# Four held-back weight tiles placed earlier in the load order of a hybrid attention block, a longer warm-up and a second cut tile

## The chip, the cores and the metric

The kernel runs on one core of one Trainium2 chip. The metric is the device time of one execution in microseconds; a median over several executions is given. One further execution was taken with the hardware profiler, and all rows shown here come from that one. TensorE (PE in the rows, with PEld for its weight loads) does the products, ScalarE (ACT) and VectorE (DVE) prepare operands and empty PSUM, and SyncE (SP) issues most DMAs.

## What is computed

One layer on an input `x` of 256 tokens by 2048 features, all in float32:

```python
proj = x @ w_in                                   # 2048 -> 5440 columns
ret_out = silu(rg) * groupnorm(retention(rope(rq), rope(rk), rv))
mla_out = mla(cq, ckv, kr)                        # latent attention with a block-causal mask
x = layer_norm(alpha * x + concat(ret_out, mla_out) @ w_out, ln1_g, ln1_b)
h = square(relu(x @ w_up)) @ w_down               # 2048 -> 8192 -> 2048
x = layer_norm(alpha * x + h, ln2_g, ln2_b)
```

## The kernel before

**Products.** Every product is made from operands split in two: a high part, rounded to the reduced float32 that TensorE takes in one pass, and a low part that holds the rest. Three products replace one: high by high, high by low, low by high. A weight tile comes from memory as a raw tile of 128 partitions by up to 2048 columns (1 MB); for each piece of 1024 columns ACT copies the high part (`L175`) and DVE subtracts it from the raw piece to get the low part (`L176`). These two instructions are "the split" of a piece, and a tile of 2048 columns has two pieces.

**Jobs.** `weights()` makes one job for each tile and appends it to the list `jobs`; the order of that list is the order of loads and of splits. `load_ahead()` issues loads, three raw buffers ahead (`NRAW`). `unit()` is called after each group of products and lets up to two pieces be split. Split pieces of most jobs go into five rotating slots (`NSLOT`), and such a piece is not emitted until the slot's former piece has been used. A job with `into=` puts its pieces into memory of its own and needs no slot. All of SP's loads stand in one queue in list order, and each waits until the raw buffer that it overwrites has been split.

**Start.** Five products on a zeroed tile `warm` run first (`L365`). The first stage takes 16 tiles `w_mla` of 1344 columns, numbered kt = 0 to 15, each in two pieces of 896 and 448 columns. Tile 0 alone is cut into three loads of 448 columns, the first of them issued by ACT, and its products stand in an order of their own (`L384`): all 12 with the high weights, column block by column block, then 6 with the low weights. All others go through `xstat` (`L286`), where the low weights are wanted after the first three products. Each tile takes 18 products of 448 columns. Between the weights, tiles of `x_t` are loaded and split too (`x_job`).

**Down projection.** 64 tiles `w_down`, kt = 0 to 63, against the squared activations `rhl`, which ACT and DVE split four tiles at a time in `r_split(b)` (`L876`, `L877`); batch b serves kt = 4b to 4b+3, and there are two buffers for batches. Tiles 0 to 57 (`NDOWN = 58`) run in order of kt, each with 24 products of 512 columns into all eight PSUM banks. The last six tiles, 58 to 63, are held back and run bank by bank (`down_bank`), 18 products for each bank, so that the final layer norm of one bank can overlap the products of the next. Tiles 58 to 61 have memory of their own (`staged_down`), 62 and 63 use the slots. In the list of jobs all stand in order of kt. `r_split(15)`, for tiles 60 to 63, is issued behind tile 57:

```python
        if kt % 4 == 1 and kt // 4 < 15:
            r_split(kt // 4 + 1)
```

After tile 63 two tiles with the rows of the last layer norm are loaded (`row_job(2)`, `row_job(3)`). Two such tiles for the first layer norm stand behind `w_down` tiles 8 and 16 in the list, and are used by DVE in four pieces each.

Of the kernel before, what the change touches and what calls it, by code (L numbers as in the profile page):

```python
# [14 lines left out]
P = 128  # L15
# [9 lines left out]
NMLA = 1344  # L25
# [9 lines left out]
NDOWN = 58  # L35
# [32 lines left out]
def kernel(  # L68
# [19 lines left out]
    nc = tc.nc  # L88
# [12 lines left out]
    def acc(name):  # L101
        return psum.tile([P, 512], F32, tag="acc", name=name)

    def bank(name):
        return psum.tile([P, 512], F32, tag="wk", name=name)
# [16 lines left out]
    def next_piece(force):  # L122
        while state["job"] < len(jobs) and jobs[state["job"]].emitted == len(jobs[state["job"]].pieces):
            state["job"] += 1
        if state["job"] == len(jobs):
            return False
        job = jobs[state["job"]]
        if job.slotted:
            if len(holders) >= NSLOT and not force and not holders[-NSLOT][0]:
                return False  # L130
            holders.append(job.free[job.emitted])
        load_ahead(state["job"])
        job.pieces[job.emitted]()
        job.emitted += 1
        return True

    def use(job, n=None):
        while job.emitted < (len(job.pieces) if n is None else n):
            next_piece(True)
        return Cols(job.hi, job.width), Cols(job.lo, job.width)  # L140

    def free(job, pieces=None):
        for i, f in enumerate(job.free):
            if pieces is None or i in pieces:
                f[0] = True

    def raw_tile(job, name):
        job.raw = wraw.tile([P, 2048], F32, tag="raw", name=name)
        return job.raw

    def weights(src, n, name, into=None, width=1024, cuts=None):

        job = Job(None, [], into is None)
        job.width = width
        spans = list(zip(cuts, cuts[1:])) if cuts else [(0, n)]

        def load():
            raw = raw_tile(job, f"raw_{name}")
            for i, (a, b) in enumerate(spans):
                (nc.scalar if cuts and i == 0 else nc.sync).dma_start(raw[:, a:b], src[:, a:b])  # L160

        def piece(i):
            a, m = i * width, min(width, n - i * width)
            if into is None:
                hi = wsp.tile([P, 1024], F32R, tag="hi", name=f"hi_{name}_{i}")
                lo = wsp.tile([P, 1024], F32R, tag="lo", name=f"lo_{name}_{i}")
            else:
                hi, lo = into(i)
            job.hi.append(hi)
            job.lo.append(lo)  # L170
            for o, e in spans if cuts else ((a, a + m),):
                o, e = max(o, a) - a, min(e, a + m) - a
                if o < e:
                    r = job.raw[:, a + o:a + e]
                    nc.scalar.copy(hi[:, o:e], r)  # L175
                    nc.vector.tensor_sub(lo[:, o:e], r, hi[:, o:e].bitcast(F32))  # L176

        job.load = load
        job.pieces = [lambda i=i: piece(i) for i in range((n + width - 1) // width)]
        job.free = [[False] for _ in job.pieces]  # L180
        jobs.append(job)
        return job

    def other(load, pieces):
        job = Job(None, pieces, False)
        job.load = lambda: load(job)
        job.free = []
        jobs.append(job)
        return job
# [14 lines left out]
    xhl = slab.tile([P, KT, 512], F32R, tag="slab", name="xhl")  # L204
# [4 lines left out]
    def x_job(k0, n):  # L209
        def load(job):  # L210
            nc.sync.dma_start(xraw[:, k0 * S:(k0 + n) * S], x_t[:, k0 * S:(k0 + n) * S])

        def piece():
            v = xraw[:, k0 * S:(k0 + n) * S].rearrange("p (k t) -> p k t", k=n)
            nc.vector.tensor_copy(xhl[:, k0:k0 + n, 0:S], v)
            nc.vector.tensor_sub(xhl[:, k0:k0 + n, S:], v, xhl[:, k0:k0 + n, 0:S].bitcast(F32))

        other(load, [piece]).raw_user = False
# [73 lines left out]
    x_job(0, 1)  # L292
    j_mla, j_ret, j_out = [], [], []
    for k in range(KT):
        j_mla.append(weights(w_mla[k], NMLA, f"mla{k}", width=896, cuts=(0, 448, 896, NMLA) if k == 0 else None))
        if k in X_AFTER:
            x_job(*X_AFTER[k])

# [11 lines left out]
    def staged_out(i):  # L310
        def into(j):
            if i == 0:
                t = work.tile([P, 2048], F32R, tag="big", name=f"wsx{j}", bufs=2)
                return t[:, 0:1024], t[:, 1024:2048]
            if "out" not in staged:
                staged["out"] = slab.tile([P, 8192], F32R, tag="slab", name="wst")
            o = (2 * i - 2 + j) * 2048
            return staged["out"][:, o:o + 1024], staged["out"][:, o + 1024:o + 2048]
        return into

    def staged_down(i):
        def into(j):
            if (i // 2, "down") not in staged:
                staged[i // 2, "down"] = slab.tile([P, 8192], F32R, tag="slab", name=f"wst{2 + i // 2}")
            o = (2 * (i % 2) + j) * 2048
            t = staged[i // 2, "down"]
            return t[:, o:o + 1024], t[:, o + 1024:o + 2048]
        return into

    for half in range(2):  # L330
        row = []
        for i in range(KT // 2):
# [3 lines left out]
                               into=staged_out(n) if half and n >= 0 else None))  # L336
        j_out.append(row)
    j_up = [weights(w_up[ft], 2048, f"wu{ft}") for ft in range(64)]
    j_down = []
    norm_rows = {}  # L340

    def row_job(i, pieces):
        def load(job):
            norm_rows[i] = raw_tile(job, f"row{i}")
            nc.sync.dma_start(norm_rows[i], ln_rows[i:i + 1].partition_broadcast(P))
        other(load, pieces)

    def x1_piece(i, tb, a):
        c = xt[:, tb, a:a + 1024]
        op = nc.vector.tensor_mul if i == 0 else nc.vector.tensor_add  # L350
        op(c, c, norm_rows[i][:, a:a + 1024])

    for kt in range(64):
        j_down.append(weights(w_down[kt], 2048, f"wd{kt}", into=staged_down(kt - NDOWN) if NDOWN <= kt < 62 else None))
        if kt in (8, 16):
            i = (8, 16).index(kt)
            row_job(i, [lambda i=i, tb=tb, a=a: x1_piece(i, tb, a) for tb in range(2) for a in (0, 1024)])
    row_job(2, [])
    row_job(3, [])


    nc.gpsimd.memset(warm, 0.0)
    am = [[acc("m0"), acc("m1"), bank("m2")], [acc("m3"), acc("m4"), bank("m5")]]
    for i in range(5):
        nc.tensor.matmul(am[1][0][:, 0:P], warm, warm, start=True, stop=True)  # L365
    MW = (448, 448, 448)
    qnT = ml[:, 0:2048].rearrange("p (h t) -> p h t", h=H)
# [8 lines left out]
    for kt in range(KT):  # L376
        hi, lo = use(j_mla[kt])
        last = kt == KT - 1
        if kt == 0:
            for fst, lst, w_part, halves in ((True, False, hi, (0, S)), (False, True, lo, (0,))):  # L380
                for j, w in enumerate(MW):
                    for tb in range(2):
                        for o in halves:
                            nc.tensor.matmul(am[tb][j][:, :w], xhl[:, 0, o + tb * P:o + (tb + 1) * P],  # L384
                                             w_part[:, j * w:(j + 1) * w], start=fst and o == 0, stop=False)
        for tb in range(2):
            if kt:
                xstat(am[tb], [(xhl, kt, hi, lo, 0)], MW, False, last, tb)
            if last:
                cp = nc.scalar.copy if tb == 0 else nc.vector.tensor_copy  # L390
                for b, w in enumerate(MW):
                    cp(lat[:, tb, b * w:(b + 1) * w], am[tb][b][:, :w])
        free(j_mla[kt])
        if kt == 5:
            side.append(constants())
        unit(3)
# [475 lines left out]
    def r_split(b):  # L872
        if b < 16:
            t = work.tile([P, 4, 512], F32R, tag="big", name="rhl", bufs=2)
            r = rr[b // 8][:, b % 8 * 4:b % 8 * 4 + 4]
            nc.scalar.copy(t[:, :, 0:S], r)  # L876
            nc.vector.tensor_sub(t[:, :, S:], r, t[:, :, 0:S].bitcast(F32))  # L877
            rhls[b] = t
# [20 lines left out]
    ad = [[(acc if j < 2 else bank)(f"d{tb}{j}") for j in range(4)] for tb in range(2)]  # L899
    for kt in range(NDOWN):  # L900
        hi, lo = use(j_down[kt])
        for tb in range(2):
            xstat(ad[tb], [(rhls[kt // 4], kt % 4, hi, lo, 0)], (512,) * 4, kt == 0, False, tb)
            if tb == 1:
                free(j_down[kt])
            unit()
        if kt % 4 == 1 and kt // 4 < 15:
            r_split(kt // 4 + 1)


# [130 lines left out]
```

## Time and profile before

| | us |
|---|---|
| median of 3 executions (lowest, highest) | 1147.86 (1146.55, 1148.38) |
| the profiled execution, its own time | 1149.33 |
| its span, first to last instruction | 1147.5 |
| PE busy in the span | 1134.4 |
| DVE busy | 690.2 |
| ACT busy | 504.4 |
| mean DMA rate over the span | 189 GB/s |

The profiled execution's own time holds 1.83 us that lie outside its span. Busy time says how long an engine had work in it; it does not say whether that work ran at the full clock, nor which engine the others waited for.

### The profile page before, as it was taken

What the parts mean: (1) busy time and instruction counts of PE and PEld (TensorE: products, weight loads), DVE (VectorE), ACT (ScalarE), POOL (GpSimd) and SP (SyncE); (2) the same over time, 40 slices, a digit from 0 to 9 for tenths busy, and PEclk for the clock granted to TensorE, in tenths of its full rate; (3) what the DMA queues carried; (4) which work ended last, traced back from release to release, by engine and by line L of the source; (5) the groups of instructions that cost most, each with busy time, mean ns of one, the idle gap of its engine ahead of it and who ended that gap; (6) DMA issues with size and microseconds to landing.
All of it is one profiled execution on the core that took longest, in us unless ns stands there. A gap on an engine that the chain in (4) does not pass through costs nothing.

```text
span 1147.5 us, 14159 instructions
## 1 busy us (share of the span) xinstructions
PE 1134.4 (99%) x5642; PEld 961.2 (84%) x5642; DVE 690.2 (60%) x922; ACT 504.4 (44%) x650; POOL 9.7 (1%) x17
## 2 busy tenths in 40 slices
PE   9999999999999999999999999999999999999988
PEld 8988888888888888888888888888888888888865
DVE  6676775666656686555555655554656455445556
ACT  4445563545453544444444444443443443344430
POOL 0000000000000000000000000000000000000000
PEclk9999999999999999999999999999999999999989
DMA  8664364435464716555555555555656555555551
GB/s 280 223 219 174 125 243 151 175 129 188 166 249 181 266 65 220 184 184 186 190 190 190 191 189 185 184 184 180 218 191 236 202 183 188 204 194 183 193 210 73
DMA packets 33761, 217.12 MB, mean 189 GB/s; under 512 B 4128, under 2 KB 5024, under 8 KB 10272
## 3 DMA queue, kind: packets, MB, share of 16 engines
q1 hardware_dynamic: 33552, 216.00, 52.9%
q8 instruction: 44, 0.72, 0.3%
q10 hardware_dynamic: 144, 0.23, 0.1%
q14 instruction: 21, 0.17, 0.0%
HBM read 214.12 MB, written 2.10 MB: 188 GB/s over the span
## 4 chain that ended last, share of the span: by engine, by line
PE 96%; DVE 1%; DMA 1%; ACT 1%; issue 0%; POOL 0%; POOLq 0%; ACTq 0%
PE d L286 29%; PE up L603 20%; PE r L286 15%; PE up L604 10%; PE o L286 7%; PE m L286 5%; PE pu L603 2%; PE pv L286 1%; PE pu L604 1%; PE pq L286 1%; DMA raw_wd<-in_w_down 1%; PE up L765 1%; PE m L384 1%; PE pms L627 0%; PE pms L626 0%; DVE wst L176 0%
## 5 line engine op out<-in xcount | busy, mean ns | idle before, releaser
L603 PE MATMUL up<-x1hl,hi_wu 128*128 128x512 f32 x984 | 347.7, 399 | 0.0
L604 PE MATMUL up<-x1hl,lo_wu 128*128 128x256 f32 x984 | 276.4, 281 | 0.0
L286 PE MATMUL d<-hi_wd,rhl 128*128 128x512 f32 x960 | 241.4, 390 | 0.0
L176 DVE TENSOR_TENSOR lo_wd<-raw_wd,hi_wd 128x1024 fp32r<-128x1024 f32 x120 | 141.9, 1222 | 151.1 <-ACT hi_wd L175 150.9
L603 PEld LDWEIGHTS up<-x1hl,hi_wu 128*128 128x128 f32 x984 | 184.9, 188 | 46.1
L286 PEld LDWEIGHTS d<-hi_wd,rhl 128*128 128x128 f32 x960 | 180.7, 188 | 37.7
L175 ACT CAST hi_wd<-raw_wd 128x1024 fp32r<-128x1024 f32 x120 | 121.1, 1054 | 182.4 <-PE d L286 175.9
L176 DVE TENSOR_TENSOR lo_wu<-raw_wu,hi_wu 128x1024 fp32r<-128x1024 f32 x128 | 156.4, 1225 | 74.2 <-ACT hi_wu L175 70.2
L604 PEld LDWEIGHTS up<-x1hl,lo_wu 128*128 128x128 f32 x984 | 185.9, 189 | 0.0
L175 ACT CAST hi_wu<-raw_wu 128x1024 fp32r<-128x1024 f32 x128 | 134.2, 1052 | 83.1 <-PE up L603 80.7
L286 PE MATMUL r<-hi_ret,xhl 128*128 128x512 f32 x512 | 147.1, 397 | 0.0
L286 PE MATMUL d<-lo_wd,rhl 128*128 128x512 f32 x480 | 130.7, 390 | 0.0
L286 PEld LDWEIGHTS r<-hi_ret,xhl 128*128 128x128 f32 x512 | 93.9, 188 | 18.2
L286 PEld LDWEIGHTS d<-lo_wd,rhl 128*128 128x128 f32 x480 | 90.4, 188 | 18.8
L176 DVE TENSOR_TENSOR lo_ret<-raw_ret,hi_ret 128x1024 fp32r<-128x1024 f32 x64 | 75.7, 1220 | 22.7 <-ACT hi_ret L175 22.5
L286 PE MATMUL r<-lo_ret,xhl 128*128 128x512 f32 x256 | 79.4, 391 | 0.0
L866 ACT COPY ut<-up 128x256 f32<-128x256 f32 x64 | 23.9, 373 | 118.8 <-PE up L604 116.1
L175 ACT CAST hi_ret<-raw_ret 128x1024 fp32r<-128x1024 f32 x64 | 64.9, 1051 | 14.4 <-PE r L286 11.6
L867 DVE TENSOR_TENSOR ut<-ut,up 128x256 f32<-128x256 f32 x64 | 27.0, 421 | 65.2 <-ACT ut L866 65.2
L286 PE MATMUL o<-hi_wo,mix 128*128 128x512 f32 x208 | 57.1, 392 | 0.0
L286 PEld LDWEIGHTS r<-lo_ret,xhl 128*128 128x128 f32 x256 | 48.0, 188 | 10.4
L286 PEld LDWEIGHTS o<-hi_wo,mix 128*128 128x128 f32 x208 | 38.7, 188 | 7.9
(192 smaller groups left out, 1021.6 us busy)
## 6 DMA issues: line engine op xcount, KB each, us to landing
raw_wu<-in_w_up SPq DMA_DIRECT2D x64, 1024.0 KB, 4.8
raw_wd<-in_w_down SPq DMA_DIRECT2D x64, 1024.0 KB, 4.8
raw_ret<-in_w_ret SPq DMA_DIRECT2D x32, 1024.0 KB, 4.8
raw_wo<-in_w_out SPq DMA_DIRECT2D x16, 1024.0 KB, 4.8
raw_mla<-in_w_mla SPq DMA_DIRECT2D x15, 672.0 KB, 5.0
raw_qk<-in_w_qk SPq DMA_DIRECT2D x8, 640.0 KB, 3.9
row<-in_ln_rows SPq DMA_DIRECT2D x4, 1024.0 KB, 4.7
raw_uv<-in_w_uv SPq DMA_DIRECT2D x2, 1024.0 KB, 4.8
```

What stands on the lines that cost most here:

```text
L175: nc.scalar.copy(hi[:, o:e], r)
L176: nc.vector.tensor_sub(lo[:, o:e], r, hi[:, o:e].bitcast(F32))
L286: nc.tensor.matmul(accs[j][:, :w], x_part, w_part[:, a:a + w], start=first and fst and i == 0, stop=last and lst and i == len(steps) - 1)
L384: nc.tensor.matmul(am[tb][j][:, :w], xhl[:, 0, o + tb * P:o + (tb + 1) * P], w_part[:, j * w:(j + 1) * w], start=fst and o == 0, stop=False)
L603: nc.tensor.matmul(pb, hi[:, a:a + P], hl[:, k0 + i], start=first and i == ks[0], stop=False)
L604: nc.tensor.matmul(pb[:, 0:S], lo[:, a:a + P], hl[:, k0 + i, 0:S], start=False, stop=last and i == ks[-1])
L765: nc.tensor.matmul(pb[:, :, t], hi[:, k * P:(k + 1) * P], x1hl[:, k].rearrange("p (a t) -> p a t", a=2)[:, :, t], start=tb == 0 and k == 0 ...
L866: nc.scalar.copy(t, pb[:, S:])
L867: nc.vector.tensor_add(t, t, pb[:, 0:S])
```

## The change

The four staged tiles 58 to 61 of the down projection are moved in the list of jobs: one stands behind each of the tiles 36, 41, 46 and 51. Tiles 62 and 63 then follow tile 57. `r_split(15)` is issued ahead of the products of tile 56 and no longer behind those of tile 57. At the start nine warm-up products run in place of five, and tile 1 of `w_mla` is cut into three loads of 448 columns and takes tile 0's order of products; all three of its loads are issued by SP, and only tile 0's first one by ACT.

```diff
         def load():
             raw = raw_tile(job, f"raw_{name}")
             for i, (a, b) in enumerate(spans):
-                (nc.scalar if cuts and i == 0 else nc.sync).dma_start(raw[:, a:b], src[:, a:b])
+                (nc.scalar if name == "mla0" and i == 0 else nc.sync).dma_start(raw[:, a:b], src[:, a:b])
...
-        j_mla.append(weights(w_mla[k], NMLA, f"mla{k}", width=896, cuts=(0, 448, 896, NMLA) if k == 0 else None))
+        j_mla.append(weights(w_mla[k], NMLA, f"mla{k}", width=896, cuts=(0, 448, 896, NMLA) if k < 2 else None))
...
-    for kt in range(64):
-        j_down.append(weights(w_down[kt], 2048, f"wd{kt}", into=staged_down(kt - NDOWN) if NDOWN <= kt < 62 else None))
+    down = {}
+    for kt in range(NDOWN):
+        down[kt] = weights(w_down[kt], 2048, f"wd{kt}")
         if kt in (8, 16):
             i = (8, 16).index(kt)
             row_job(i, [lambda i=i, tb=tb, a=a: x1_piece(i, tb, a) for tb in range(2) for a in (0, 1024)])
+        if kt in (36, 41, 46, 51):
+            i = (36, 41, 46, 51).index(kt)
+            down[NDOWN + i] = weights(w_down[NDOWN + i], 2048, f"wd{NDOWN + i}", into=staged_down(i))
+    for kt in (62, 63):
+        down[kt] = weights(w_down[kt], 2048, f"wd{kt}")
+    j_down = [down[kt] for kt in range(64)]
     row_job(2, [])
     row_job(3, [])
...
-    for i in range(5):
+    for i in range(9):
         nc.tensor.matmul(am[1][0][:, 0:P], warm, warm, start=True, stop=True)
...
-        if kt == 0:
+        if kt < 2:
             for fst, lst, w_part, halves in ((True, False, hi, (0, S)), (False, True, lo, (0,))):
                 for j, w in enumerate(MW):
                     for tb in range(2):
                         for o in halves:
-                            nc.tensor.matmul(am[tb][j][:, :w], xhl[:, 0, o + tb * P:o + (tb + 1) * P],
-                                             w_part[:, j * w:(j + 1) * w], start=fst and o == 0, stop=False)
+                            nc.tensor.matmul(am[tb][j][:, :w], xhl[:, kt, o + tb * P:o + (tb + 1) * P],
+                                             w_part[:, j * w:(j + 1) * w],
+                                             start=kt == 0 and fst and o == 0, stop=False)
         for tb in range(2):
-            if kt:
+            if kt >= 2:
                 xstat(am[tb], [(xhl, kt, hi, lo, 0)], MW, False, last, tb)
...
     for kt in range(NDOWN):
         hi, lo = use(j_down[kt])
+        if kt == NDOWN - 2:
+            r_split(15)
         for tb in range(2):
             xstat(ad[tb], [(rhls[kt // 4], kt % 4, hi, lo, 0)], (512,) * 4, kt == 0, False, tb)
             if tb == 1:
                 free(j_down[kt])
             unit()
-        if kt % 4 == 1 and kt // 4 < 15:
+        if kt % 4 == 1 and kt // 4 < 14:
             r_split(kt // 4 + 1)
```

## Rows read from the trace of the kernel before

**Rows 1.** The page's busy times: us, share of the span, instructions of each engine.

```profile
PE 1134.4 (99%) x5642; PEld 961.2 (84%) x5642; DVE 690.2 (60%) x922; ACT 504.4 (44%) x650; POOL 9.7 (1%) x17
```

**Rows 2.** Chain of waits, 900 us to the end: start us, us, what set the time.

```profile
899.82 185.65 PE d L286 x819
...
1092.38 7.09 DMA raw_wd<-in_w_down
```

**Rows 3.** Timeline, 1085 to 1137 us: start us, us, engine, line, operation, [idle before, releaser].

```profile
1086.45 3.90 ACT L175 CAST wst<-raw_wd 128x1024 fp32r<-128x1024 f32 x4
...
1096.41 1.32 PEld L286 LDWEIGHTS d<-wst,rhl 128*128 128x128 f32 x6
...
1100.52 1.04 ACT L876 CAST rhl<-rr 128x1024 fp32r<-128x1024 f32 x1
...
1101.61 0.73 PE L286 MATMUL d<-wst,rhl 128*128 128x512 f32 x2 [3.46 <-ACT rhl L876]
...
1103.06 2.07 PE L286 MATMUL d<-wst,rhl 128*128 128x512 f32 x4 [0.72 <-DVE rhl L877]
...
1118.99 0.19 PEld L286 LDWEIGHTS d<-hi_wd,rhl 128*128 128x128 f32 x1
...
1123.07 0.19 PEld L286 LDWEIGHTS d<-hi_wd,rhl 128*128 128x128 f32 x1
...
1136.67 0.41 PEld L947 LDWEIGHTS sh<-row,ident 128*128 128x128 f32 x2
```

**Rows 4.** Windows: stretch, its us; PE, PEld, DVE, ACT, POOL busy; PEclk; DMA; GB/s.

```profile
1102.00:1103.00 1.00, 0.34 (x2) 0.00 (x0) 1.00 (x2) 1.00 (x2) 0.00 (x0) 0.71 0.97 410
1103.00:1109.00 6.00, 5.94 (x14) 4.69 (x15) 4.65 (x6) 1.40 (x2) 0.00 (x0) 0.50 0.63 249
1109.00:1110.00 1.00, 1.00 (x5) 0.78 (x5) 0.15 (x1) 0.00 (x0) 0.00 (x0) 0.87 0.00 0
```

**Rows 5.** The page's costliest groups: xcount, busy us, mean ns, idle before and its releaser.

```profile
L176 DVE TENSOR_TENSOR lo_wd<-raw_wd,hi_wd 128x1024 fp32r<-128x1024 f32 x120 | 141.9, 1222 | 151.1 <-ACT hi_wd L175 150.9
```

**Rows 6.** The tile raw_wd, 790 to 1080 us: its 53 DMAs, issue to landing.

```profile
DMA to landing us min/median/max: 4.6/4.8/5.5
```

**Rows 7.** Timeline of ACT where the list has a row tile (815 to 830 us).

```profile
820.80 1.06 ACT L175 CAST hi_wd<-raw_wd 128x1024 fp32r<-128x1024 f32 x1 [0.80 <-DMA raw_wd<-in_w_down]
```

**Rows 8.** Windows, one stretch around the same row tile; columns as in rows 4.

```profile
815.00:835.00 20.00, 20.00 (x90) 16.57 (x89) 14.61 (x13) 7.68 (x8) 0.00 (x0) 1.00 0.67 237
```

**Rows 9.** Timeline of the first 13 us.

```profile
0.99 2.50 PE L365 MATMUL m<-warm 128*128 128x128 f32 x10 [0.99 <-POOL warm L362]
...
1.18 0.90 SPq L160 DMA_DIRECT2D raw_mla<-in_w_mla  x2
...
4.45 1.72 ACT L175 CAST hi_mla<-raw_mla 128x448 fp32r<-128x448 f32 x3 [2.00 <-DMA raw_mla<-in_w_mla]
...
5.07 4.85 PE L384 MATMUL m<-hi_mla,xhl 128*128 128x448 f32 x12 [1.58 <-ACT hi_mla L175]
...
9.20 1.41 ACT L175 CAST hi_mla<-raw_mla 128x896 fp32r<-128x896 f32 x2 [3.03 <-DMA raw_mla<-in_w_mla]
...
9.72 1.58 PE L384 MATMUL m<-lo_mla,xhl 128*128 128x448 f32 x6
...
11.14 0.77 PE L286 MATMUL m<-hi_mla,xhl 128*128 128x448 f32 x3
...
11.50 1.41 ACT L175 CAST hi_mla<-raw_mla 128x896 fp32r<-128x896 f32 x2 [0.89 <-DMA raw_mla<-in_w_mla]
...
12.36 1.38 PE L286 MATMUL m<-hi_mla,xhl 128*128 128x448 f32 x6
```

**Rows 10.** DMA issues of the first 30 us: count, KB each, median us to landing.

```profile
raw_mla<-in_w_mla SPq DMA_DIRECT2D x9, 672.0 KB, 5.6
...
raw_mla<-in_w_mla SPq DMA_DIRECT2D x2, 224.0 KB, 3.9
```

More of the change, by code (lines that the diff above doesn't have):

```diff
@@ L338 @@
     j_up = [weights(w_up[ft], 2048, f"wu{ft}") for ft in range(64)]
-    j_down = []
     norm_rows = {}
```

## Prediction

> **What bounds the kernel now.** I read four views. The page's busy times first: PE has work in 1134.4 of 1147.5 us [rows 1], so no other engine's share is worth anything by itself; to be won are only stretches in which PE stands or runs slowly. The chain of waits second, to find where it leaves PE: before 1085 us it stays there for 185.65 us, and then goes through DVE and ACT splits and a wait of 7.09 us for a load of `w_down` [rows 2]. The timeline third. PE has finished tile 57 at 1096.41 and does the six products of tiles 58 and 59; for tile 60 it needs `r_split(15)`. That copy stands in ACT's queue behind the split of tile 62, whose raw tile lands only at 1092.38 + 7.09 = 1099.47. So the copy starts at 1100.52, and PE stands for 3.46 us, and 0.72 us more for DVE's half of the split [rows 2, 3]. Why is tile 62 late? Tiles 58 to 61 need no slot, so their splits go out in one run (four casts back to back from 1086.45 [rows 3]); each raw buffer comes free late, and the loads of 61 to 63 follow as fast as the queue allows but not fast enough.
>
> The windows last: after the stop the granted clock is 0.71 in one microsecond, 0.50 for six, 0.87 in the next [rows 4]. So PE fell to the lower of its two levels (1.2 of 2.4 GHz) at about 1102.4 and came back at about 1109.3, 6.2 us after it had begun to work without a stop at 1103.06 [rows 3].
>
> **The end: what the change removes.** Undisturbed, a bank's 18 products take 1123.07 - 1118.99 = 4.08 us, or 0.227 us each [rows 3]. Eight banks are 32.6 us. From 1096.41 to the first product of `L947` at 1136.67 it took 40.26 us [rows 3]. The end thus loses 7.62 us: 3.46 + 0.72 = 4.18 standing, and 3.44 at the lower clock.
>
> After the change nothing is late at this place. At 24 products of 0.227 us a tile takes 5.44 us, so tile 55 ends at 1096.41 - 10.88 = 1085.5. `r_split(15)` follows there, behind two pieces (57's second, 62's first): three casts of 1.05 and three DVE halves of 1.22 us [rows 3, 5] make it ready by about 1085.5 + 1.05 + 3 x 1.22 = 1090.2; PE wants it at 1097.8. Its buffer is that of batch 13, last read by tile 55, so only ACT waits. Tiles 62 and 63 load when tiles 55 and 56 before them in the list are split, some 1078.1 and 1083.5; with the usual 4.8 us [rows 6] they land at 1082.9 and 1088.3, and are cast from 1086.5 and 1092. 63's second piece must wait for a slot until 1096.4, and is wanted by bank 2 at 1104.6. The two row tiles move forward in SP's queue as well: they wait for the splits of 57 and 62 (1087.8 and 1093.3) and land by about 1098; the first layer norm needs them after 16 us of banks. So I take the whole 7.62 us. Bounds: 4.18 if the clock falls anyway, 7.62.
>
> **The four tiles in the middle.** Each insertion adds, within one tile's time, two casts (2.1 us) and two DVE halves (2.4 us) to the two that ACT and DVE do in any case: 4.2 and 4.9 of 5.44 us. At the last of the four `r_split(13)` falls in the same place: ACT 5.3, DVE 6.1 us, 0.7 over, against pieces emitted 10.9 us ahead of use. SP's queue gets one more 1 MB load; the tile behind it loads one buffer later than usual: it lands 2.3 + 4.8 = 7.1 us after the freeing of a tile, is split by 9.4, and is wanted at 16.3. Behind a late cast on ACT stand only later casts and a batch that has 10 us. The memory of these tiles was last read by the up projection and by `r_split(7)`, both over before 930 us. The trace holds the same insertion: the row tile in the list near 820 us. ACT waited 0.80 us for a load there and PE not at all, 20.00 of 20.00 us busy [rows 7, 8]. Cost: nothing; without this cover, a load's 4.8 us each time. The low bound is nothing as well: PE had no stop there to give back.
>
> **The start.** The column of the clock shows 1.00 here, but no record covers these microseconds; the level must be read from the beat. The 12 high products run from 5.07 to 9.72, 0.388 us each. From 11.14 to 12.36 it is 6 products, 0.203 each [rows 9]: half the clock before, the full one after. Six low products in 9.72 to 11.14 fit one or two slow ones, so the clock rose near 10.1, 5.0 us after the work at 5.07 began. The warm-up ran from 0.99 and left PE idle for 1.58 us before that [rows 9].
>
> Nine warm-up products are 18 entries instead of 10. At 2.50 / 10 = 0.25 us at most [rows 9] they end by 5.5, at 0.21 (leaving out the drain of the last) by 4.8: they fill the idle 1.58 us and delay the first product by 0 to 0.4; I take 0.05, since entries follow closer than their modelled ends. Work is then unbroken from 0.99. If the rise comes 5.0 to 6.2 us after its beginning, as at the two places seen, it comes at 6.0 to 7.2. The 13 products that now run slowly (5.03 / 0.388) would then take 0.93 + 10.6 x 0.203 = 3.1 or 2.1 + 7.5 x 0.203 = 3.65 us instead of 5.03: 1.4 to 1.95 us won. A page of the Trainium skill (TensorE: Matmul & The Clock Gate, "What's actually happening") says that the number of slow products at a kernel's start differs between runs of one kernel. No row of a single execution shows that; by it this term would differ from run to run, and the sum stays as it is.
>
> Can the data keep up? Tile 1's products would begin at 9.5 instead of 11.14. Its raw tile lands at 9.20, and a cast of 448 columns takes 0.57 us (1.72 / 3) [rows 9]: 9.8 if the first third lands no sooner than the whole does now. Cut, it should land sooner, and the new order asks for the second and third block 0.8 and 1.6 us later and for low weights only after 2.4. SP spends two more issues, 0.9 us [rows 9]; behind them stand `x_t` and tile 2. Tile 2 is wanted at 11.14 + 18 x 0.203 = 14.8 now, 13.2 then; cast from 11.50, done 12.9, or 13.8 if the 0.9 counted in full, and the third block is wanted only 0.4 after the first. One more cast and one more DVE half cost 0.3 us off PE's path. I put 0.1 against all this and take 1.5 for the start, with bounds 0 (the clock rises no sooner, or data bind) and 1.95.
>
> A rule speaks against the cut. The DMA landings show 3.9 us for a piece of 224 KB against 5.6 for a tile of 672 KB [rows 10]: pieces cost more per byte, and yet tile 0's three were cast back to back within 1.72 us of 4.45 [rows 9], so they overlap. The Trainium skill (DMA: Bandwidth & Descriptors, "Anatomy of one DMA") gives each DMA some 2 us of fixed cost, stated for another issuing engine; if pieces paid it in turn, an estimate from that page of the Trainium skill is 4 us more for tile 1, PE would stand 2.6 us for its last third, and the start would lose 1.1 us instead of winning 1.5. By the trace of tile 0 they don't pay in turn.
>
> **Sum.** 7.62 + 1.5 = 9.1 us. The profiled execution's own time is 1149.33 (span 1147.5 and 1.83 around it): 1140.2. It stands 1.47 above the median of the runs shown; against that median the sum gives 1138.7. Of the 1.47 no row tells the cause. If other executions lose less at the end's lower clock, the median already holds less of it to win. I take the middle, **1139.5 us**.
>
> **Rivals.**
> The start gives nothing (clock rise unmoved, or PE then waits for tile 1 or 2): 1139.5 + 1.5 = 1141.0. For it: no row shows the start's clock directly, and warm-up products are small. Against: at both places the rise followed on unbroken work.
> Tile 1's thirds land one after another: 3 x 3.9 = 11.7 against 5.6 us, 6.1 late at worst. The last would be cast by 15.9, against 11.2 wanted: 4.7 us of standing, 1144.2. Against it: tile 0. By the estimate from the Trainium skill (DMA: Bandwidth & Descriptors) it would be 1139.5 + 2.6 = 1142.1.
> The stop at the end stays: tile 62 again lands late (7.09 as now, or later) and holds `r_split(15)` on ACT. It would need to be 7.6 us behind the times above; price 4.2, with the clock 7.6: 1143.7 to 1147.1, the latter not to be told from before. Against: the slack of 3.7 us ahead of the cast.
> Slower: each inserted load holds up the tile behind it until PE stands. The place is tiles 38, 43, 48 and 53; it decides once each stop costs over 9.1 / 4 = 2.3 us, that is once a tile lands 6.9 + 2.3 = 9.2 us later than worked out, 14 us after issue, against 5.5 as the longest seen [rows 6]. With 4 us each: 1139.5 + 16 = 1155.5.
>
> **How the numbers follow.** Forecast 0.78, the start gives nothing 0.12, thirds in turn 0.04, the stop stays 0.04 (half of it within the bound), slower 0.02. Faster by over 0.2% (2.3 us, about what a measurement of this kernel can tell) is then 0.96, same 0.02, slower 0.02. The range: at the low end 1147.86 - 7.62 - 1.95 = 1138.3, less the 1.3 by which the fastest run lies below the median: 1137.0. At the high end the own time less the end's 7.62 alone: 1141.7. It holds the first two cases.
>
> **What would show it.** Right: in the timeline, PE's products of tile 60 follow those of 59 without idle time, eight banks take 32.6 us, the windows show clock 1.00 up to the last bank; ACT casts into `wst` stand near 971, 998, 1025 and 1053 us, with no PE wait beside them; at the start the beat falls to 0.203 us near 6 to 7 us, and tile 1 begins near 9.5. Wrong: PE idle in the middle, a new wait at `r_split(15)` or a beat of 0.388 until 10.

## The result and the profile after

The changed kernel takes 1140.76 us (median of 6, 1140.25 to 1141.73) against 1147.65 (6 executions, 1146.55 to 1148.90) of the kernel before. The ratio is 0.9941 with a 95% interval of 0.9929 to 0.9954: 6.8 us less by the ratio, between 5.3 and 8.1. The forecast was 1139.5 with a range of 1137.0 to 1141.7. The profiled execution takes 1141.47, its span is 1139.5 us; against the profiled execution before that is 7.9 us, against a sum of 9.1.

The busy times of the page after, against [rows 1]: PE has 2.4 us less work in a span that is 8.0 us shorter.

```profile
PE 1132.0 (99%) x5650; PEld 959.0 (84%) x5650; DVE 690.5 (61%) x923; ACT 504.7 (44%) x651; POOL 9.7 (1%) x17
```

**The end.** The timeline of the changed kernel, 1086 to 1129 us, with the lines that answer to [rows 3]:

```profile
1086.87 1.05 ACT L883 CAST rhl<-rr 128x1024 fp32r<-128x1024 f32 x1
...
1088.33 1.22 DVE L884 TENSOR_TENSOR rhl<-rr,rhl 128x1024 fp32r<-128x1024 f32 x1
...
1095.88 2.68 PEld L286 LDWEIGHTS d<-wst,rhl 128*128 128x128 f32 x12
...
1128.52 0.41 PEld L956 LDWEIGHTS sh<-row,ident 128*128 128x128 f32 x2
```

The batch is cast at 1086.87, nine microseconds before tile 58, and its low part is ready at 1088.33 + 1.22 = 1089.55, where 1090.2 was forecast. The 12 weight loads of tiles 58 to 61 now stand in one run, where [rows 3] had six, a stop, two, a stop, four. The shift product (`sh`, `L947` before, `L956` now) is the first product behind the eight banks. From the first load of tile 58 to the load of the shift product it is 1128.52 - 1095.88 = 32.64 us, against 40.26 before. The windows (columns as in [rows 4]) show the same stretch and the down projection ahead of it:

```profile
790.00:1095.00 305.00, 305.00 (x1348) 252.54 (x1347) 167.49 (x143) 135.01 (x135) 0.00 (x0) 1.00 0.60 215
...
1096.00:1129.00 33.00, 33.00 (x147) 27.28 (x146) 19.11 (x29) 0.90 (x1) 0.91 (x1) 1.00 0.09 33
```

PE is busy for the whole of both, at the full clock.

**The inserted tiles.** ACT's timeline at the first of the four (the casts into `wst` begin at 971.68, and at the other three at 998.88, 1026.09 and 1053.29):

```profile
970.73 1.05 ACT L175 CAST hi_wd<-raw_wd 128x1024 fp32r<-128x1024 f32 x1 [2.49 <-PE d L286]
971.68 2.00 ACT L175 CAST wst<-raw_wd 128x1024 fp32r<-128x1024 f32 x2
973.59 1.04 ACT L175 CAST hi_wd<-raw_wd 128x1024 fp32r<-128x1024 f32 x1
...
978.08 1.05 ACT L175 CAST hi_wd<-raw_wd 128x1024 fp32r<-128x1024 f32 x1 [0.85 <-DMA raw_wd<-in_w_down]
```

Four casts in one run, and one wait of 0.85 us for the load behind them, as at the row tile of [rows 7]. The next insertions wait 0.73, 0.82 and 0.70 us. All of it is ACT's time; PE, in the window above, has none of it.

**The start.** The timeline of the first 17 us, against [rows 9]:

```profile
0.99 4.21 PE L371 MATMUL m<-warm 128*128 128x128 f32 x18 [0.99 <-POOL warm L368]
...
5.17 2.98 PE L390 MATMUL m<-hi_mla,xhl 128*128 128x448 f32 x12
...
6.99 1.73 ACT L175 CAST hi_mla<-raw_mla 128x448 fp32r<-128x448 f32 x3 [0.74 <-DMA raw_mla<-in_w_mla]
...
7.99 1.40 PE L390 MATMUL m<-lo_mla,xhl 128*128 128x448 f32 x6
...
9.23 2.64 PE L390 MATMUL m<-hi_mla,xhl 128*128 128x448 f32 x12
...
13.67 0.30 PEld L286 LDWEIGHTS m<-lo_mla,xhl 128*128 128x128 f32 x2 [0.33 <-DVE lo_mla L176]
...
14.51 1.40 PE L286 MATMUL m<-hi_mla,xhl 128*128 128x448 f32 x6
...
16.37 1.40 PE L286 MATMUL m<-hi_mla,xhl 128*128 128x448 f32 x6
```

The twelve high products take 7.99 - 5.17 = 2.82 us instead of 4.65. The beat, the time from the start of one product to the start of the next, is 0.2067 us behind them, and twelve at this beat would take 2.48. So the clock rose during the first of them, and tile 1 begins at 9.23 and not at 11.14. The thirds of tile 1 are cast from 6.99, 2.2 us earlier than the whole was. At 13.67 PE's weight load has waited 0.33 us for the low part of tile 2, and the next one waits 0.23 us more. And from 14.51 to 16.37 nine products take 1.86 us, 0.2067 each, where [rows 9] has 0.203. So the lead of 1.9 us shrinks: the next stage begins at 65.35 us against 65.86, and the start has brought 0.5 us in this execution.

**The rest.** What is left of the own time beside the stretch up to the load of the shift product is 1149.33 - 1136.67 = 12.66 us before and 1141.47 - 1128.52 = 12.95 now. About half of the 0.29 us between them lies behind that load within the span (10.8 and 11.0 us), the other half outside the span (1.83 and 1.97). It was in no term of the forecast. With it the two profiled executions add up: 0.51 won at the start and 7.62 at the end, less 0.29, is 7.84 of the 7.86 us between them.

### The profile page after: what moved, and what is told of

It is laid out like the page before. It is cut to its first block, busy times and chain, and to the rows that moved or that the text cites. A ratio compares the mean times of both kernels' runs of the same rounds, so it can differ in the third digit from the quotient of the medians.

```text
span 1139.5 us, 14182 instructions
## 1 busy us (share of the span) xinstructions
PE 1132.0 (99%) x5650; PEld 959.0 (84%) x5650; DVE 690.5 (61%) x923; ACT 504.7 (44%) x651; POOL 9.7 (1%) x17
## 4 chain that ended last, share of the span: by engine, by line
PE 98%; DVE 1%; ACT 0%; POOL 0%; POOLq 0%; issue 0%; ACTq 0%
PE d L286 31%; PE up L610 20%; PE r L286 15%; PE up L611 10%; PE o L286 7%; PE m L286 5%; PE pu L610 2%; PE pv L286 1%; PE pu L611 1%; PE pq L286 1%; PE m L390 1%; PE up L772 1%; PE pms L634 0%; PE pms L633 0%; PE m L371 0%; PE up L780 0%
```

## The experiments

The kernels were timed in three groups, each with its own executions of the kernel before: the medians of before are 1146.77 (24 executions; the first four experiments), 1147.44 (9; the changed kernel a second time, tile 1 whole, tile 2 cut, other column blocks) and 1146.59 (15; the kernel before once more, the changed kernel a third time, five warm-up products, tile 2 cut again). A kernel is compared with before by its ratio, and the gain in us is that ratio put to the median of before; kernels of one group are compared by their medians.

**The end alone.** The list and the batch as in the change, the start as before (five warm-up products, tile 0 alone cut).

```diff
-    for kt in range(64):
-        j_down.append(...)
+    for kt in range(NDOWN):
+        down[kt] = ...                     # 58 to 61 behind 36, 41, 46, 51
...
+        if kt == NDOWN - 2:
+            r_split(15)
```

> Both parts of the end (tiles 58 to 61 moved in the list, batch 15 split ahead of tile 56), the start as before. Theory: the end is worth 7.6 us in a profiled execution and nearly the whole of the change, since the start won 1.9 us and gave 1.4 of them back; so about 1141.2 us against 1147.7 before, PE without idle time from tile 0 of the down projection to the last bank, and the clock at its upper level there. Rival: the end is worth only its 4.2 us of standing in executions without the profiler, and the rest of the 6.9 us comes from the start: about 1143.5. On the side: the products of 448 columns in the first stage have a beat of 0.203 us (as before, if the start decides it) or 0.207 (if it is chance).

Measured: 1141.94 us, ratio 0.9953 (0.9942 to 0.9965), 5.4 us less. First load of tile 58 to the shift product: 32.63 us, no PE wait from 780 to 1128 us. The end is most of the change in medians, but less than the 7.6 of the profiled execution; it lies between the theory's 6.5 and the rival's 4.2, both inside the interval (4.0 to 6.6), and so doesn't decide by itself.

**The start alone.** List and batch as before.

```diff
-    for i in range(5):
+    for i in range(9):
...
-cuts=(0, 448, 896, NMLA) if k == 0 else None
+cuts=(0, 448, 896, NMLA) if k < 2 else None
...
-        if kt == 0:
+        if kt < 2:
```

> Nine warm-up products and tile 1 in thirds with its new order of products; the end as before. Theory: the clock rises near 5.2 us and PE is 1.9 us ahead after tile 0, loses 0.56 to the low part of tile 2 and 0.9 to a beat of 0.207 us: 0.5 us net, about 1147.1 us, the same as before within the noise; the stop of 3.5 us at the end is still there. Rival: in most executions the beat is the faster one, and the start keeps 1.4 us: about 1146.2. Second rival: the start is worth the 2.7 us that the first experiment's rival needs: about 1145.

Measured: 1145.70 us, ratio 0.9989 (0.998 to 0.9997), 1.3 us less (0.3 to 2.3). That is nearest to the first rival; the interval holds the theory's 0.5 as well, and not the 2.7 of the second rival. Its timeline:

```profile
5.13 3.40 PE L384 MATMUL m<-hi_mla,xhl 128*128 128x448 f32 x12
...
9.58 2.59 PE L384 MATMUL m<-hi_mla,xhl 128*128 128x448 f32 x12
...
14.45 1.38 PE L286 MATMUL m<-hi_mla,xhl 128*128 128x448 f32 x6
...
16.27 1.38 PE L286 MATMUL m<-hi_mla,xhl 128*128 128x448 f32 x6
...
64.30 0.63 PE L286 MATMUL r<-hi_ret,xhl 128*128 128x512 f32 x2
...
1094.82 1.32 PEld L286 LDWEIGHTS d<-wst,rhl 128*128 128x128 f32 x6
...
1098.68 1.03 PE L286 MATMUL d<-wst,rhl 128*128 128x512 f32 x2 [2.12 <-ACT rhl L877]
...
1100.13 2.07 PE L286 MATMUL d<-wst,rhl 128*128 128x512 f32 x4 [0.42 <-DVE rhl L878]
...
1131.89 0.41 PEld L948 LDWEIGHTS sh<-row,ident 128*128 128x128 f32 x2
```

```profile
1098.00:1099.00 1.00, 0.32 (x1) 0.30 (x2) 1.00 (x2) 1.00 (x2) 0.00 (x0) 0.97 1.03 418
1099.00:1102.00 3.00, 2.58 (x7) 1.49 (x5) 3.00 (x3) 2.46 (x3) 0.00 (x0) 0.50 0.71 295
1102.00:1103.00 1.00, 1.00 (x5) 0.85 (x4) 1.00 (x2) 0.00 (x0) 0.00 (x0) 0.83 0.87 229
```

Here nine products take 1.82 us, no low part is late, and the next stage begins 1.56 us earlier than in the kernel before. The same start had given 0.5 in the execution above. The stop at the end is still there, as expected, but it is 2.12 and 0.42 us here and the clock is low for 3.4 us (1098.94 to 1102.34): the end takes 1131.89 - 1094.82 = 37.07 us and loses 4.4, where the same end lost 7.6 in the first profile of the kernel before. 5.4 + 1.3 = 6.7: the two halves of the change add up to the whole, within intervals of some 2 us.

**The list alone.** The start as before, and of the end only this:

```diff
+        if kt in (36, 41, 46, 51):
+            i = (36, 41, 46, 51).index(kt)
+            down[NDOWN + i] = weights(w_down[NDOWN + i], 2048, f"wd{NDOWN + i}", into=staged_down(i))
```

> Tiles 58 to 61 moved in the list, batch 15 still split behind tile 57, the start as before. Theory: no load is late any more, but the batch stands behind the second piece of tile 63 on ACT and DVE and begins only when tile 57 ends; PE waits some 0.7 us for the high part and 1 us for the low part, too little to lower the clock: about 1.7 us above the version with both parts, 1142.9 us. Rival: the batch is hidden by the products of tiles 58 and 59 and moving it is worth nothing: equal to the version with both parts.

Measured: 1144.24 us, ratio 0.9973 (0.9962 to 0.9984), 2.3 us above the version with both. PE's products around the batch:

```profile
1099.53 0.73 PE L286 MATMUL d<-wst,rhl 128*128 128x512 f32 x2 [0.28 <-ACT rhl L883]
...
1100.98 1.19 PE L286 MATMUL d<-wst,rhl 128*128 128x512 f32 x4 [0.71 <-DVE rhl L884]
```

The waits stand where they were expected and are shorter, 1.0 us together; with smaller gaps around them it is 1.55 us over the eight banks (34.19 against 32.64), and the clock stayed at 1.00. The two profiled executions are 3.23 us apart (1144.36 and 1141.13): the other 1.66 us are in the first stage, which ended later here (66.96 against 65.30) with the same start; this execution has the slower of the two beats, 0.2067 us, and the other 0.203. How the 2.3 us between the medians divide is not shown.

**The batch alone.** The start and the list as before, and of the end only this:

```diff
+        if kt == NDOWN - 2:
+            r_split(15)
...
-        if kt % 4 == 1 and kt // 4 < 15:
+        if kt % 4 == 1 and kt // 4 < 14:
```

> Batch 15 split ahead of tile 56, the four tiles where they were in the list, the start as before. Theory: PE no longer stands for the batch but for the high and low parts of tiles 62 and 63, whose loads are as late as before; bank 0 ends near 1105 us instead of 1100.5 without a wait, so 4 to 5 us are still lost: about 1145 us. Rival: only the batch was in the way, and PE meets ready tiles behind it: about 1141.2 us, as with both parts.

Measured: 1147.96 us, ratio 1.0009 (1.0000 to 1.0017). Neither number was right: the batch alone brings nothing. PE's timeline, and the windows:

```profile
1100.85 0.50 PE L286 MATMUL d<-lo_wd,rhl 128*128 128x512 f32 x1 [0.77 <-DVE lo_wd L176]
...
1102.11 0.50 PE L286 MATMUL d<-hi_wd,rhl 128*128 128x512 f32 x1 [0.53 <-ACT hi_wd L175]
1103.37 0.79 PE L286 MATMUL d<-lo_wd,rhl 128*128 128x512 f32 x1 [0.76 <-DVE lo_wd L176]
```

```profile
1102.00:1103.00 1.00, 0.50 (x1) 0.19 (x1) 0.91 (x1) 1.00 (x2) 0.00 (x0) 0.81 0.96 385
1103.00:1109.00 6.00, 5.63 (x13) 4.46 (x14) 2.83 (x4) 0.01 (x1) 0.00 (x0) 0.50 0.48 201
1109.00:1110.00 1.00, 1.00 (x5) 0.75 (x4) 0.00 (x0) 0.00 (x0) 0.00 (x0) 0.78 0.00 0
```

The mechanism was the expected one, PE waits for tiles 62 and 63 in place of the batch. But waits of 0.8 us at most were enough to bring the clock down. A granted clock of 0.81 from 1102 to 1103 puts its fall at 1102.6, when the waits of 0.77 and 0.53 us were over and the third began. It stayed low for 6.8 us, as behind the one stop of 3.46 us in [rows 4], and the eight banks take 38.72 us, 6.1 more than without a wait.

**The kernel before, once more.**

> The kernel before, profiled once more. Theory: the stop at the end is there in every execution (about 3.5 and 0.7 us of standing), but the stretch at the lower clock behind it differs: 6.8 us in the first profiled execution and in that with the batch alone, 3.4 us in that with the new start alone; a shorter one makes the end cost near 5.9 instead of 7.6 us, and explains why the gain in medians (6.6 to 6.9 us) is less than between the profiled executions (7.9). Rival: the stretch is 6.8 us again and the profiled execution is near 1149, so the difference of 1.5 us lies elsewhere, in the first stage or outside the span.

Its median is 1147.53 us (11 executions), ratio 1.0003 (0.9994 to 1.0012). Its profiled execution takes 1148.48 us, span 1146.7. Timeline and windows:

```profile
1097.50 1.32 PEld L286 LDWEIGHTS d<-wst,rhl 128*128 128x128 f32 x6
...
1102.05 0.73 PE L286 MATMUL d<-wst,rhl 128*128 128x512 f32 x2 [2.81 <-ACT rhl L876]
...
1103.50 1.80 PE L286 MATMUL d<-wst,rhl 128*128 128x512 f32 x4 [0.72 <-DVE rhl L877]
...
1135.83 0.41 PEld L947 LDWEIGHTS sh<-row,ident 128*128 128x128 f32 x2
```

```profile
1100.00:1105.00 5.00, 2.23 (x6) 1.56 (x7) 4.81 (x5) 4.83 (x5) 0.00 (x0) 0.88 0.86 326
1105.00:1106.00 1.00, 1.00 (x4) 0.72 (x4) 1.00 (x2) 0.00 (x0) 0.00 (x0) 0.50 0.80 131
1106.00:1107.00 1.00, 1.00 (x4) 0.81 (x3) 0.85 (x1) 0.00 (x0) 0.00 (x0) 0.50 0.61 254
1107.00:1110.00 3.00, 3.00 (x15) 2.43 (x14) 1.38 (x2) 0.00 (x0) 0.00 (x0) 0.96 0.54 221
```

The theory holds. The stop is 3.5 us in all instead of 4.2, the clock is low from 1103.8 to 1107.3, and the end takes 1135.83 - 1097.50 = 38.33 us: 5.7 us lost, not 7.6, of which the clock is 2.2 instead of 3.4. The execution is only 0.85 us faster than the first one all the same, since the stage behind the first one begins 0.30 us later (66.16) and the stretch from there to tile 58 is 0.8 us longer; PE waits 0.62 us near 410 us, at the first layer norm, where the first execution shows no wait. So what the change removes at the end differs from one execution to the next, standing and clock both: 7.6, 5.7 and, with the new start, 4.4 us. The spread agrees: 3.9 us over the 24 executions of before in the first group (1145.32 to 1149.21), 2.2 over all 16 of the changed kernel (1139.95 to 1142.13).

**The changed kernel twice more,** as it is.

> The changed kernel itself once more, as the base for the others of this call. Theory: the beat of the first stage's products is not set by the change but differs from one execution to the next (0.203 or 0.207 us); the median stays near 1140.8 us, and stage one of the profiled execution ends near 64.4 us with the fast beat or near 65.4 with the slow one. Rival: the change itself brings the slow beat; then it shows 0.207 again.

> The changed kernel a third time, as the base of this call: about 1140.8 us, with the waits of about 0.5 us for tile 2's low part and either beat behind them.

Measured: 1140.87 us, ratio 0.9943 (0.993 to 0.9957), and 1140.33, ratio 0.9942 (0.993 to 0.9955). PE's timeline in the first of them:

```profile
8.96 2.60 PE L390 MATMUL m<-hi_mla,xhl 128*128 128x448 f32 x12
...
12.62 0.77 PE L286 MATMUL m<-hi_mla,xhl 128*128 128x448 f32 x3
13.50 1.01 PE L286 MATMUL m<-lo_mla,xhl 128*128 128x448 f32 x3
14.35 1.40 PE L286 MATMUL m<-hi_mla,xhl 128*128 128x448 f32 x6
...
16.21 1.40 PE L286 MATMUL m<-hi_mla,xhl 128*128 128x448 f32 x6
```

Tile 1's 18 products take 12.62 - 8.96 = 3.66 us, 0.203 each. Then comes the wait for tile 2's low part, and behind it nine products take 1.86 us, 0.2067 each, to the end of the stage at 65.19. In the other execution the beat behind the same wait is 0.203 and the stage ends at 64.00. So the beat belongs neither to the change nor to a whole execution. Here it changed behind a wait; whether the wait changes it is not shown, since it stayed the same behind the same wait in the other two executions.

**Warm-up and cut taken apart.** The changed kernel with five warm-up products:

```diff
-    for i in range(9):
+    for i in range(5):
```

and, in a kernel of its own, with tile 1 whole:

```diff
-cuts=(0, 448, 896, NMLA) if k < 2 else None
+cuts=(0, 448, 896, NMLA) if k == 0 else None
...
-        if kt < 2:
+        if kt == 0:
...
-            if kt >= 2:
+            if kt:
```

> The changed kernel with five warm-up products again; tile 1 still in thirds. Theory: the warm-up is what moves the clock: the first products run at 0.373 us until near 9 to 10 us, tile 3 begins near 18 us as with the end alone, and the time is 0.5 to 1.5 us above the changed kernel, 1141.5 to 1142.3. Rival: the cut tile, not the warm-up, gave the start its gain: then the same time as the changed kernel.

> The changed kernel with tile 1 loaded and multiplied as before (one load, the old order of products). Theory: tile 0's products end near 9.2 us, tile 1's high part is there only near 10.1 and its low part near 11.2, so PE waits about 1 us; half of it is not lost, since tile 2 held PE up anyway: 0.5 us above the changed kernel. Rival: tile 1 in one load is just as early as in three, or tile 2 takes back everything: no difference in where tile 3 begins.

Five warm-up products: 1142.82 us, 2.5 above the changed kernel of the same group and more than the 0.5 to 1.5 expected (its profile has the slower beat), ratio to before 0.9961 (0.9948 to 0.9973). Tile 1 whole: 1141.09 us, ratio 0.9944 (0.9931 to 0.9956), 0.2 above the changed kernel of its group. With five:

```profile
5.12 4.85 PE L390 MATMUL m<-hi_mla,xhl 128*128 128x448 f32 x12 [1.62 <-ACT hi_mla L175]
9.76 1.54 PE L390 MATMUL m<-lo_mla,xhl 128*128 128x448 f32 x6
```

With tile 1 whole:

```profile
5.11 3.02 PE L390 MATMUL m<-hi_mla,xhl 128*128 128x448 f32 x12
...
9.79 0.93 PE L286 MATMUL m<-hi_mla,xhl 128*128 128x448 f32 x3 [0.42 <-ACT hi_mla L175]
10.91 1.00 PE L286 MATMUL m<-lo_mla,xhl 128*128 128x448 f32 x3 [0.19 <-DVE lo_mla L176]
```

Five products bring the lower clock back for the whole of tile 0's high part (4.64 us), nine take it away whatever tile 1 does. The warm-up is the start's gain. In execution times the cut of tile 1 is worth nothing that can be told (0.2 us). The profiles show why that is little: the whole tile makes PE wait, and at the faster beat the next stage begins at 65.26 with it (one execution) and at 64.00 and 64.30 with the thirds. But the cut costs something elsewhere. The rest of the own time, as in the section on the result, is 12.65 or 12.66 us in the six profiled executions with tile 1 whole (the kernel before twice, the end, the list and the batch alone, and this one), and 12.94 to 12.97 in the five with tiles 0 and 1 in thirds (the changed kernel three times, the start alone, and five warm-up products). So 0.3 us are paid back there, and no run shows by what. What the cut is worth in all stays open, between nothing and about 1 us.

**A cut of tile 2 as well,** run twice.

```diff
-cuts=(0, 448, 896, NMLA) if k < 2 else None
+cuts=(0, 448, 896, NMLA) if k < 3 else None
...
-        if kt < 2:
+        if kt < 3:
...
-            if kt >= 2:
+            if kt >= 3:
```

> The changed kernel with tile 2 of the first stage cut into thirds and ordered like tiles 0 and 1. Theory: the two waits for tile 2's low part (0.56 us) go, since low weights are wanted 2.4 us later; tile 3 begins up to 0.5 us earlier where the clock rises early, nothing where it rises late: 0 to 0.5 us faster. Rival: two more issues on SP delay tile 3 and the x tiles, and the wait moves to tile 3 or 4: no change or up to 0.5 us slower.

> The version with tiles 0 to 2 in thirds once more, beside the changed kernel in the same call. Theory: it is 0.5 to 0.8 us faster than the changed kernel, since PE no longer waits for tile 2's low part; about 1140.1. The beat behind it may be either one. Rival: the 0.8 us of the first comparison were the beat's chance, and the two medians lie within 0.3 us of each other.

Measured: 1140.07 us beside 1140.87 of the changed kernel in the second group, 1140.88 beside 1140.33 in the third; ratios to before 0.9936 (0.9924 to 0.9949) and 0.9945 (0.9932 to 0.9957). The wait for the low part is gone in both, but the second comparison goes the other way by 0.55 us, so the 0.8 us can't be told from chance. The rest of the own time is 13.01 and 12.84 us here. No version here is measurably faster than the changed kernel.

**Other column blocks.** The 1344 columns in blocks of 512, 512 and 320.

```diff
-    MW = (448, 448, 448)
+    MW, MO = (512, 512, 320), (0, 512, 1024)
```

With it go cuts at 512 and 1024, pieces of 1024 and 320 columns, and the column offsets that follow from `MO`.

> The changed kernel with the 1344 columns of the first stage's products in blocks of 512, 512 and 320 where it had three of 448 (pieces of 1024 and 320 columns, cuts at 512 and 1024). Theory: the two beats belong to 448 columns; 512 take 0.227 us as in the down projection and 320 about 0.147, 0.601 for three against 0.608 or 0.620: the first stage ends 0.7 us sooner than with the fast beat and 1.8 sooner than with the slow one, and every execution has the same beat: 1139.5 to 1140 us. Rival: a third of the products is then shorter than their weight loads of 0.188 us and runs at that pace, 0.642 for three: 2 to 3 us slower in the first stage.

Measured: 1141.17 us, ratio 0.9945 (0.9933 to 0.9958). Its timeline:

```profile
13.29 0.77 PE L286 MATMUL m<-hi_mla,xhl 128*128 128x512 f32 x3
13.89 0.78 PE L286 MATMUL m<-lo_mla,xhl 128*128 128x512 f32 x3
14.51 1.40 PE L286 MATMUL m<-hi_mla,xhl 128*128 128x512 f32 x6
```

The theory is wrong, and so is the rival's size: from 14.51 on nine products take 1.86 us again (14.51, 16.36, 18.22 in the timeline), 0.62 for three. Up to 13.89 three take 0.60, so both beats appear here too, and the change from one to the other at 13.89 has no wait of PE beside it. The mean beat isn't a matter of 448 columns alone.

## Why the prediction was right, and where it was off

**The end, 7.62 us: right for the execution that it was read from.** 40.26 - 32.64 = 7.62 us between the two first profiles. The second profile of the kernel before gives 5.7, that of the start alone 4.4, and the end alone 5.4 (4.0 to 6.6) in medians. The step that was off is that one execution's loss was taken whole. Both its terms are too large for the other executions: the 3.44 us at the lower clock were 2.2 in the second profile and 1.9 with the start alone, and the 4.18 us of standing were 3.5 and 2.5. The prediction saw that the median might hold less of the clock's part and put its number between its two readings of the sum; that took off too little. All else in it held: batch, tiles 62 and 63 and the rows were ready, and both moves are needed. The list alone leaves 1.55 us in the banks, the batch alone brings nothing.

**The four tiles, cost nothing: right.** PE was busy for 305.00 of 305 us; ACT's waits for loads of 0.70 to 0.85 us are those of the row tile. The slower rival had no stop at any of the four.

**The start, 1.5 us: right on the average, partly by luck.** The beginning of the next stage, read in the timeline of each profile, gives the clearest number:

| start | next stage begins at, us | mean |
|---|---|---|
| five warm-up products (before twice, the end alone, list alone, batch alone, five with a cut) | 65.86, 66.16, 65.30, 66.96, 65.90, 66.94 | 66.19 |
| nine, tile 1 in thirds (changed kernel three times, the start alone) | 65.35, 65.19, 64.00, 64.30 | 64.71 |

That is 1.5 us. The beat mixes in: two in each row have the slower one, and compared at one beat it is 65.81 against 64.15 and 66.95 against 65.27, 1.7 us each. Of this the 0.3 us in the rest of the own time go off again, and 1.4 us are left, which the start alone bears out (1.3). In parts: the clock rose sooner than was forecast in the three executions of the changed kernel (tile 1 begins at 8.82 to 9.23, with the start alone at 9.58, where 9.5 was forecast; at 10.58 to 11.18 with five products), the warm-up delayed nothing, and the low part of tile 2 took more than the 0.1 us allowed (0.56 in the first profile). The working had followed tile 2 only as far as its casts on ACT, and not to its low part on DVE. That an earlier clock, a late low part and the 0.3 us come to the forecast's 1.5 is luck in the size; that the longer warm-up moves the clock is shown. The remark in the Trainium skill (TensorE: Matmul & The Clock Gate, "What's actually happening") that the number of slow products differs between runs of one kernel is borne out: the twelve first products took 2.82, 2.54 and 2.54 us in three executions of the changed kernel, and 4.65 and 3.92 in two of the kernel before.

**The thirds.** They do not land in turn: three casts in 1.73 us from 6.99. The estimate from the Trainium skill (DMA: Bandwidth & Descriptors, "Anatomy of one DMA") of 4 us more for the tile is not what the trace shows; it came sooner.

**The sum.** From 1147.65 the forecast's 1139.5 is 8.2 us less; measured are 6.8 by the ratio. The end alone gave 5.4 where 7.6 stood, the start alone 1.3 where 1.5 stood, so the difference lies in the end's term, as far as these intervals of some 2 us can tell. For the profiled execution's own time the sum gave 1140.2, and 1141.47 was measured; there the end was right, the start lacked 1.0 of its 1.5, and the other 0.3 are those in the rest of the own time, which the sum didn't have.

What stays open: why the first stage's products take one of two beats (the blocks of 512 and 320 show that it isn't 448 columns alone, and no run here picks the beat); why the stop at the end is shorter in some executions; and why the cut of tile 1 lengthens the rest of the own time.

## What to carry to other kernels

When work is held back for the end, look at what else the end does in a row: loads and splits that need no slot pile up there unless the list spreads them, and the next tile in the queue pays. Undo each half of such a change by itself: here each half of the end alone left PE waiting, and the batch alone brought nothing, since PE then stood for the next tiles, and small waits brought the clock down for as long as a big one did. Profile a kernel twice before a gain is read from one stop and the stretch at a lower clock behind it, since both differ between executions of the same code. And add up the whole execution, not only the places that were changed: the cut at the start lengthened the rest by 0.3 us.

## What the runs showed of the hardware

The granted clock fell at the end behind one stop of 3.46 us [rows 3], of 2.81 us (the kernel before once more) and of 2.12 us (the start alone), and also behind two waits of 0.77 and 0.53 us with a third just beginning (the batch alone). It didn't fall behind waits of 0.28 and 0.71 us (the list alone). The lower level (0.50, 1.2 of 2.4 GHz) lasted 6.8 us in the first profile of the kernel before and in that of the batch alone, and 3.4 us in the second profile of the kernel before (1103.8 to 1107.3) and in that of the start alone.

At the full clock the same products of 448 columns run at 0.203 us or at 0.2067 us each, for some 50 us on end; over the 246 products left in the stage at 14.51 that is 1 us. Both beats were seen with either start. The beat changed within one execution behind a wait of PE, and with blocks of 512 and 320 columns with no wait beside the change.
